# A two-layer hybrid diffusion backbone: the modulation products on the tensor engine's four column groups, the norm sums as matmuls, and a reordered start of each layer

## The chip, the core and the metric

One core of a Trainium2 chip runs the whole program. The metric is the device time of one execution in microseconds, as the median of several runs. The engines are called by the profile's names: PE (TensorE, with its weight loads as PEld), DVE (VectorE), ACT (ScalarE), POOL (GpSimd) and SP (SyncE, which only issues transfers).

## The reference, cut to what matters

There are two layers over 256 context tokens and 1024 latent tokens of width 1024. At the head of a layer each token is normalised and modulated by a vector that comes from a conditioning vector `c` (latent) or `c_ctx` (context). Three head groups then read the same projected input.

```python
for layer in range(DEPTH):                       # DEPTH = 2
    mod_x = jax.nn.silu(c) @ ada_w[layer] + ada_b[layer]        # 1024 -> 3072
    mod_c = jax.nn.silu(c_ctx) @ ada_w[layer] + ada_b[layer]
    sh_x, sc_x, gt_x = jnp.split(mod_x[:, None, :], 3, axis=-1)  # and the same of mod_c
    h_x = rmsnorm(x, norm_w[layer]) * (1.0 + sc_x) + sh_x
    h_c = rmsnorm(xc, norm_w[layer]) * (1.0 + sc_c) + sh_c
    y_x, y_c = hybrid_mixer(h_x, h_c, w_in[layer], ...)          # attention, GLA, HGRN2, out
    x = x + gt_x * y_x
    if layer < DEPTH - 1: xc = xc + gt_c * y_c
return rmsnorm(x, final_norm_w)
```

The modulation products are matrix-vector products: two vectors (`c` and `c_ctx`) times a 1024 x 3072 matrix for each layer, 12.6 MB of weights each.

## The kernel before, in words

Activations lie transposed: 8 tiles of 128 features (`KT`) by 1280 tokens (`NT`), the tokens in three chunks, A0 (256 context tokens), A1 and B (512 latent tokens each). `make_h` turns `x` into the modulated `h` as a pair, `hhi` rounded to the fast matmul format and `hlo` the remainder. A projection (`proj`) is three matmuls per feature tile (`hhi` by `whi`, `hlo` by `whi`, `hhi` by `wlo`), so 24 for a chunk and a block of 128 columns. The weights are split the same way by `split_w` on ACT and then DVE or POOL.

PE and SP run in the order in which the program is written. For DVE, ACT and POOL a scheduler sets the order at build time; each engine then runs its list in order. Most large tiles come from one pool of 34 slots ("big").

The start of layer 0: SP loads four rows of modulation weights (`ada_load`, 2.1 MB each, 512 columns), the first weights, and then `x`. `ada_row` multiplies a row on PE with `sil` (the two SiLU vectors, 2 columns) as the stationary operand into 2 partitions of `adps`, ACT copies it to `rows`, and `ada_cols` turns it into columns by matmuls with a 2 x 2 identity. The norm sums: ACT squares `x`, DVE and POOL add the squares into `acc` and `acc2` (`stats`), and `rstd` sums over partitions with one or two matmuls with a matrix of ones (`ssps`); `newton` refines the reciprocal root on ACT and DVE.

Then `gla` runs for the layer. Its small projection `gkp` and its blocks q, k, v and v2 are computed at once, chunk by chunk; after each chunk `run_side(SIDE)` takes three steps of `ada_side`, which computes the other modulation products: those of layer 1, needed only when layer 0 is done. Before the change these are 48 products of 128 x 1024 elements with a reduction, two thirds as one DVE instruction each (line 175), one third as a POOL product (line 171) and an ACT sum (line 172). `mids` is a list of steps that `gla` takes between its projections: in layer 0 the norm and `h` of chunk B and the two remaining rows of layer 0's modulation, in layer 1 the norm and `h` of chunk B (`mid_h`).

After q, k, v and v2 the scan of `gla` starts. From there on PE takes projections of later groups as fillers between the scan's steps; the first filler is the first PE work behind v2. The whole order of PE after that point is the same program before and after the change.

Of the kernel before, what the change touches and what calls it, by code (L numbers as in the profile page):

```python
# [65 lines left out]
def hybrid_kernel(ctx: ExitStack, tc: tile.TileContext, a: dict, out: bass.AP):  # L66
# [79 lines left out]
    sbc = [big(f"sbc{v}") for v in range(2)]  # L146
# [7 lines left out]
    def sbc_load():  # L154
        for v in range(2):
            cb, sv = big("cb")[:, 0:1024], sbc[v][:, 0:1024]
            nc.sync.dma_start(cb, a["cvec"][v].partition_broadcast(P))
# [4 lines left out]

    def ada_side():
        sbc_load()
        for i in range(8, 32):
# [833 lines left out]
    sil = const.tile([P, KT, 2], F32, name="sil")  # L999
    sigmul(sil, cvec)  # L1000
    xs = [big(f"x{k}") for k in range(KT)]
    adw = []
    def ada_load(i):
        w = []
        for j in range(4):
            w.append(big("adw0")[:, 0:1024].rearrange("p (k x) -> p k x", k=2))
            nc.sync.dma_start(w[j], a["ada_w"][i][:, 2 * j:2 * j + 2])
        return w

    for i in range(4):  # L1010
        adw.append(ada_load(i))
# [6 lines left out]
    rowt = big("rows")  # L1018
    rows = [rowt[0:2, 512 * (i % 2):512 * (i % 2) + 512] for i in range(6)]

    acc2 = big("acc2")

    def stats(c, xs=xs, acc=acc, acc2=acc2):
# [3 lines left out]
    def ada_cols(i):  # L1027
        pt = pst.tile([P, 512], F32, tag="t1", name="adtp")
        for j in range(4):
            nc.tensor.matmul(  # L1030
                pt[:, 2 * j:2 * j + 2], rows[i][:, j * P:(j + 1) * P], ident[0:2, 0:2], start=True, stop=True
            )
        if i < 4:
            m, b, d = m0, adab, (KT if i % 2 == 0 else 0) + 4 * (i // 2)
        else:
            m, b, d = m1, adab2, 4 * (i - 4)
        nc.vector.tensor_tensor(
            m[:, d:d + 4, :], pt[:, 0:8].rearrange("p (j v) -> p j v", v=2),
            b[:, d:d + 4].unsqueeze(2).to_broadcast([P, 4, 2]), op=ALU.add,
        )  # L1040

    def ada_row(i, w):
        ps = psp.tile([P, 512], F32, tag="pp", name="adps")
        for j in range(KT):
            nc.tensor.matmul(ps[0:2, :], sil[:, j, :], w[j // 2][:, j % 2, :], start=(j == 0), stop=(j == KT - 1))
        nc.scalar.copy(rows[i], ps[0:2, :])

    for i in range(4):
        ada_row(i, adw[i])
        if i > 0:  # L1050
            ada_cols(i - 1)
        if i in (1, 3):
            stats(CH_ALL[i // 2])
    rstd(r, acc, CH_ALL[0:1], acc2)
    ada_cols(3)
    hh = [big(f"hhi{k}", F32R) for k in range(KT)]
    hl = [big(f"hlo{k}", F32R) for k in range(KT)]
    As = [mod_gain(0, k, m0) for k in range(KT)]
    for k in range(KT):
# [4 lines left out]

    def starts(xs=xs, r=r, acc=acc, As=As, hh=hh, hl=hl):
        stats(CH_ALL[2])
        rstd(r, acc, CH_ALL[2:3], acc2)
        ada_row(4, ada_load(4))
        for k in range(KT):
# [310 lines left out]
```

## Time and profile before

| | us |
|---|---|
| median of 3 runs | 2010.65 |
| the runs | 2006.82, 2010.65, 2015.01 |
| span of the profiled execution, first to last instruction | 2006.4 |

The profile gives the span of one execution and not a time of its own beside it. It lies 0.4 us under the fastest run and 4.2 us under the median, so within the spread of the runs the span stands for the time. Over the span PE is busy 89%, DVE 68%, ACT 55% and POOL 27%. PE is the engine to watch: from about 200 us on it is busy nine tenths of the time or more in almost every slice, and the slices in which it is not lie at the start. The granted clock of PE has two levels, 2.4 and 1.2 GHz; a stretch with a share of 0.64 was at the lower level for most of its time. "Idle before" and a releaser in brackets say what an engine waited for.

### The profile page before, as it was taken

To read this page: it belongs to the slowest core of one execution; us is meant where nothing else is said; L and a number is where in the kernel's file an instruction comes from. 1 tells how busy PE (TensorE), PEld (TensorE's weight loads), DVE (VectorE), ACT (ScalarE), POOL (GpSimd) and SP (SyncE) were. 2 spreads that over 40 slices of the span, in tenths; PEclk is the share of its full clock that TensorE was granted. 3 is DMA by queue.
4 is the path that set the end of the run, shared out by engine and by line. 5 is a ranking of instruction groups with operands and counts; after the bars stand their busy time and mean duration, and the time that the engine had idled before them with its cause. 6 is when DMAs were issued, how large, how long until landed. Compare 5 with 4: busy or idle time off the path is not lost. (4 is left out here: it accounts for less than half of the span.)

```text
span 2006.4 us, 30011 instructions
## 1 busy us (share of the span) xinstructions
PE 1790.1 (89%) x10528; PEld 1408.4 (70%) x10528; DVE 1361.9 (68%) x2999; ACT 1105.6 (55%) x2891; POOL 543.3 (27%) x614
## 2 busy tenths in 40 slices
PE   7847898988989999997998988988898999999895
PEld 2436666766767788886887775666675777887775
DVE  2899847759475477678767666575838366677756
ACT  3634666457365367677634346545626355767633
POOL 1276223234243001111111333223434201111112
PEclk9878999989989999998999989999998999999997
DMA  9442112112114114416243011211211414246322
GB/s 337 151 149 100 38 48 95 48 46 85 63 42 119 48 61 115 143 64 196 96 150 129 26 40 45 84 49 48 98 66 50 114 51 119 79 123 198 102 94 84
DMA packets 81526, 190.28 MB, mean 95 GB/s; under 512 B 9408, under 2 KB 19904, under 8 KB 81376
## 3 DMA queue, kind: packets, MB, share of 16 engines
q1 hardware_dynamic: 44752, 101.72, 15.7%
q10 hardware_dynamic: 27936, 49.56, 6.8%
q0 software_dynamic: 8688, 37.10, 6.3%
q8 instruction: 83, 1.36, 0.3%
q14 instruction: 67, 0.55, 0.1%
HBM read 132.37 MB, written 45.48 MB: 89 GB/s over the span
## 5 line engine op out<-in xcount | busy, mean ns | idle before, releaser
L299 PE MATMUL pj<-hhi,whi 128*128 128x512 f32 (+1 forms) x1416 | 578.1, 408 | 8.5 <-ACT sg L317 5.7
L301 PE MATMUL pj<-hhi,wlo 128*128 128x512 f32 (+1 forms) x1416 | 536.5, 379 | 13.9 <-DVE wlo L276 11.4
L300 PE MATMUL pj<-hlo,whi 128*128 128x512 f32 (+1 forms) x1416 | 536.8, 379 | 0.0
L299 PEld LDWEIGHTS pj<-hhi,whi 128*128 128x128 f32 x1416 | 275.6, 195 | 73.9 <-issue 25.0
L301 PEld LDWEIGHTS pj<-hhi,wlo 128*128 128x128 f32 x1416 | 276.3, 195 | 70.4 <-DVE wlo L276 12.0
L300 PEld LDWEIGHTS pj<-hlo,whi 128*128 128x128 f32 x1416 | 276.5, 195 | 36.8 <-issue 2.7
L276 POOL TENSOR_TENSOR wlo<-wst,whi 128x512 fp32r<-128x512 f32 x80 | 112.9, 1412 | 494.7 <-ACT whi L275 456.1
L275 ACT CAST whi<-wst 128x512 fp32r<-128x512 f32 x144 | 84.4, 618 | 139.6 <-PE pj L300 99.6
L960 DVE TENSOR_TENSOR PT<-ptp,PT 128x384 fp32r<-128x384 f32 (+2 forms) x272 | 119.4, 466 | 34.9 <-ACT PT L959 32.8
L943 DVE CUSTOM_DVE_ANT_0 sp<-sps,tab 128x640 f32<-128x640 f32 (+2 forms) x144 | 107.4, 746 | 44.5 <-PE sps L937 41.7
L959 ACT CAST PT<-ptp 128x384 fp32r<-128x384 f32 (+2 forms) x272 | 101.6, 409 | 61.9 <-PE ptp L957 58.9
L944 ACT ACTIVATE sp<-sp,mn 128x640 f32<-128x640 f32 (+2 forms) x144 | 111.5, 774 | 41.1 <-DVE mn L943 39.5
L957 PE MATMUL ptp<-cst,sp 128*128 128x128 f32 x640 | 101.1, 282 | 19.8 <-DVE PT L960 8.1
L957 PEld LDWEIGHTS ptp<-cst,sp 128*128 128x128 f32 x640 | 78.1, 144 | 40.7 <-DVE PT L960 9.7
L970 PE MATMUL pv<-PT,nv 128*128 128x256 f32 x640 | 105.2, 293 | 0.0
L936 PE MATMUL sps<-k,q 128*128 128x256 f32 (+1 forms) x272 | 86.5, 323 | 11.9 <-DVE mn L943 11.3
L276 DVE TENSOR_TENSOR wlo<-wst,whi 128x512 fp32r<-128x512 f32 x64 | 53.5, 836 | 63.2 <-ACT whi L275 62.7
L970 PEld LDWEIGHTS pv<-PT,nv 128*128 128x128 f32 x640 | 91.0, 192 | 6.4
L317 ACT ACTIVATE sg<-pj 128x512 f32<-128x512 f32 (+1 forms) x90 | 47.9, 533 | 83.0 <-PE pj L301 82.6
L1146 DVE SCALAR_TENSOR_TENSOR xn<-py,m,xn 128x512 f32<-128x512 f32 (+1 forms) x88 | 56.9, 650 | 39.9 <-PE py L1141 38.3
L937 PE MATMUL sps<-k,q 128*128 128x256 f32 (+1 forms) x272 | 78.9, 309 | 0.0
L574 ACT COPY zg<-swg 32x64 f32<-32x64 f32 x216 | 52.0, 241 | 32.4 <-PE lv L589 24.0
(303 smaller groups left out, 3893.0 us busy)
## 6 DMA issues: line engine op xcount, KB each, us to landing
wst<-in_w_in SPq DMA_DIRECT2D x128, 256.0 KB, 3.1
pre<-sg ACTq DMA_DIRECT2D x80, 256.0 KB, 2.0
adw<-in_ada_w SPq DMA_DIRECT2D x24, 512.0 KB, 9.9
adw<-in_ada_wt SPq DMA_DIRECT2D x24, 512.0 KB, 3.5
k<-k POOLq DMA_DIRECT2D x32, 320.0 KB, 4.4
tab<-in_rpbt SPq DMA_DIRECT2D x16, 640.0 KB, 6.0
wst<-in_w_out SPq DMA_DIRECT2D x32, 256.0 KB, 3.5
oscr<-sg ACTq DMA_DIRECT2D x24, 256.0 KB, 2.0
```

The costliest lines, as they stand in the source:

```text
L275: nc.scalar.copy(hi, st)
L276: (nc.vector, nc.gpsimd)[WPOOL[h]].tensor_tensor(lo, st, fence(hi), op=ALU.subtract)
L299: nc.tensor.matmul(ps[:, :n], hi[:, k, :], mv(hh[k]), start=(k == 0), stop=False)
L300: nc.tensor.matmul(ps[:, :n], hi[:, k, :], mv(hl[k]), start=False, stop=False)
L301: nc.tensor.matmul(ps[:, :n], lo[:, k, :], mv(hh[k]), start=False, stop=(k == KT - 1))
L936: nc.tensor.matmul(sps[:, pc:pc + w], Q1[h][:, qc:qc + P], K1[h][:, kc:kc + w], start=True, stop=False)
L943: nc.vector.tensor_tensor_reduce(sp, sps[:, c0:c0 + n], tab[:, tb:tb + n], -1.0, 3.0e38, ALU.add, ALU.min, mn)
L944: nc.scalar.activation(sp, sp, AF.Exp, bias=mn, scale=-1.0, accum_out=sm)
L957: nc.tensor.transpose(pt[:, j * P:(j + 1) * P], sp[:, (b0 + j) * P:(b0 + j + 1) * P], ident)
L959: nc.scalar.copy(PT[:, b0:b0 + bn, 0, :], p3)
L960: nc.vector.tensor_tensor(PT[:, b0:b0 + bn, 1, :], p3, fence(PT[:, b0:b0 + bn, 0, :]), op=ALU.subtract)
L970: nc.tensor.matmul(pv[:, i % 2], V[h][:, c, :], st[i]["PT"][:, j], start=(j == 0), stop=(j == len(chs) - 1))
```

## The change

It does five things.

1. `ada_side` multiplies on PE. A step loads a chunk of 256 columns (`ada_w2`, two transfers of 0.5 MB), and `ada_mm` does 8 matmuls with 32 stationary columns each (2 of the vectors, 30 zeros), feature tile j into the column group 32 * (j % 4) of `adps`, so that four groups hold four partial sums. ACT copies 128 x 256 to `rows`, and `ada_fold` sums the groups and turns the row into columns with 2 matmuls against `sel`. There are 16 chunks: layer 1's modulation and the last third of layer 0's, which had been rows 4 and 5 of `mids`. The DVE, POOL and ACT products are gone.
2. Layer 0's first four rows use `ada_mm` and `ada_fold` with 512 columns.
3. `stats` sums the squares on PE: 8 matmuls with the matrix of ones per chunk in place of additions on DVE and POOL.
4. ACT's queue issues the loads of chunks A0 and A1 of `x`, A0 ahead of the first modulation row, A1 behind it; chunk B stays on SP behind the weights. Two of the eight feature tiles of `h` in layer 0 (`HPOOL0`) take a product and a subtraction on POOL.
5. `gla` projects chunk A0 of q and k before `gkp` of chunk A1, takes the second step of `mids` only after q of chunk A1, and has k's weights loaded ahead of time. This holds for layer 1 too.

```diff
-    sbc = [big(f"sbc{v}") for v in range(2)]
+    rowt = big("rows")
+    sil = rowt[:, 1024:1280].rearrange("p (k x) -> p k x", x=32)
+    nc.gpsimd.memset(sil, 0.0)
...
+    def ada_mm(ps, ws, n):
+        for j in range(KT):
+            g = 32 * (j % 4)
+            nc.tensor.matmul(
+                ps[g:g + 32, :n], sil[:, j, :], ws[j], start=(j < 4), stop=(j >= 4), skip_group_check=True
+            )
+
+    def ada_fold(row, n, m, b, d):
+        pt = pst.tile([P, 512], F32, tag="t1", name="adtp")
+        w = n // P
+        for j in range(w):
+            nc.tensor.matmul(pt[:, 2 * j:2 * j + 2], row[:, j * P:(j + 1) * P], sel, start=True, stop=True)
...
     def ada_side():
-        sbc_load()
-        for i in range(8, 32):
-            w = big("adw")[:, 0:1024]
-            nc.sync.dma_start(w, a["ada_wt"][i - 8])
-            for v in range(2):
-                if (2 * i + v) % ADAM < ADAP:
-                    t = big("adt")[:, 0:1024]
-                    nc.gpsimd.tensor_tensor(t, w, sbc[v][:, 0:1024], op=ALU.mult)
-                    nc.scalar.activation(t, t, AF.Copy, accum_out=m1[:, i, v:v + 1])
-                else:
-                    t = sgt().bitcast(BF16)
-                    nc.vector.scalar_tensor_tensor(
-                        t, w, 1.0, sbc[v][:, 0:1024], op0=ALU.mult, op1=ALU.mult, accum_out=m1[:, i, v:v + 1]
-                    )
...
+        ws = load(0)
+        for c in range(16):
+            nxt = load(c + 1) if c < 15 else None
+            ps = psp.tile([P, 512], F32, tag="pp", name="adps")
+            ada_mm(ps, ws, 256)
+            row = rowt[:, 256 * (c % 4):256 * (c % 4) + 256]
+            nc.scalar.copy(row, ps[:, 0:256])
             yield
+            ada_fold(row, 256, m1, adab2, 2 * c)
+            ws = nxt
+            yield
...
         gkp(CH_A[0:1])
         next(mids)
+        if CH_A[0] in chunks:
+            run(wq, CH_A[0:1], q, sq)
+        run(wk, CH_A[0:1], k)
         gkp(CH_A[1:2])
+        run(wq, CH_A[1:2], q, sq)
         next(mids)
-        wk = load_split(a["w_in"][l, GLK])
-        run(wq, [c for c in chunks if c in CH_A], q, sq)
-        next(mids, None)
-        run(wk, CH_A, k)
+        run(wk, CH_A[1:2], k)
         gkp(CH_B)
...
+    x_load(nc.scalar, 0)
+    adw = [ada_load(0)]
+    x_load(nc.scalar, 1)
+    adw += [ada_load(i) for i in (1, 2, 3)]
     pw = gla_weights(0)
-    for s, n in CH_ALL:
-        for k in range(KT):
-            nc.sync.dma_start(xs[k][:, s:s + n], a["xin"][:, k, s:s + n])
+    x_load(nc.sync, 2)
...
+    def stats(c, acc=acc, r=r, xs=xs):
+        s, n = CH_ALL[c]
+        ps = pst.tile([P, 512], F32, tag="t1", name="ssps")
         for k in range(KT):
-            stat((acc, acc2)[k % 2], xs[k], k // 2, *c, eng=(nc.vector, nc.gpsimd)[k % 2])
+            sq = sgt()[:, :n]
+            nc.scalar.activation(sq, xs[k][:, s:s + n], AF.Square)
+            nc.tensor.matmul(ps[:, :n], ones, sq, start=(k == 0), stop=(k == KT - 1))
...
+    stats(0)
+    row = ada_row(0)
+    stats(1)
+    for i in range(4):
+        nrow = ada_row(i + 1) if i < 3 else None
+        ada_fold(row, 512, m0, adab, (KT if i % 2 == 0 else 0) + 4 * (i // 2))
+        row = nrow
+        if i % 2 == 1:
+            ks = range(2 * (i - 1), 2 * (i - 1) + 4)
+            for k in ks:
+                As[k] = mod_gain(0, k, m0)
+            h_part(0, ks)
+    h_part(1, range(KT))
```

The order of ACT at the very start, before:

```order
L1366 UNCONDITIONAL_BRANCH
L231 ACT_TABLE_LOAD
L149 ACTIVATE sil<-smalls 128x16
L134 ACTIVATE lbe<-lbe 128x8
L1046 COPY rows<-adps 2x512 x2
L708 CAST wg<-gkst 128x8x32
L275 CAST whi<-wst 128x512
```

and with the change (rows 9 to 21 of its list; the first loads of chunk A0 stand ahead of them):

```order
L1019 DMA x_125<-in_xin 128x256
L1019 DMA x_126<-in_xin 128x256
L1019 DMA x_127<-in_xin 128x256
L1019 DMA x_120<-in_xin 128x512
L1019 DMA x_121<-in_xin 128x512
L1019 DMA x_122<-in_xin 128x512
L1019 DMA x_123<-in_xin 128x512
L1019 DMA x_124<-in_xin 128x512
L1019 DMA x_125<-in_xin 128x512
L1019 DMA x_126<-in_xin 128x512
L1019 DMA x_127<-in_xin 128x512
L1042 ACTIVATE sg<-x_120 128x256
```

All sixteen loads of chunks A0 and A1 now stand ahead of ACT's first square (line 1042), and PE's first matmul needs that square.

On PE behind the first projection of q (chunk A0) in layer 0, with the change; `adps` is a chunk's product, `adtp` its fold:

```order
L314 MATMUL pj<-hhi_219,wlo 128x256
L159 MATMUL adps<-adw,rows 32x256 x8
L167 MATMUL adtp<-smalls,rows 128x2 x2
L159 MATMUL adps<-adw,rows 32x256 x8
L312 MATMUL pj<-hhi_212,whi 128x256
```

where DVE, in the same stretch of the program before the change, had the products (line 175) between the work of `gla` itself (`glf` and `glk` are its decay and its key):

```order
L276 TENSOR_TENSOR wlo<-wst,whi 128x512
L744 TENSOR_TENSOR glf_957<-glf_957,glu 128x256
L175 SCALAR_TENSOR_TENSOR sg,m_111<-adw,sbc_113 128x1024
L175 SCALAR_TENSOR_TENSOR sg,m_111<-adw,sbc_114 128x1024
L743 TENSOR_SCALAR glf_957<-zps,smalls 128x512
L765 TENSOR_TENSOR glk_413<-glk_413,rsh 128x1024
```

The products have left DVE's list, and PE's has a product and a fold directly behind one another, with ACT's copy of the product between them.

On PE in layer 1, around the norm sum of chunk B (`ssps`), before:

```order
L720 MATMUL pj<-hhi_10160,wg 128x512
L721 MATMUL pj<-hlo_10168,wg 128x512
L202 MATMUL ssps<-acc,cst 128x512
L299 MATMUL pj<-hhi_10153,whi 128x512
L300 MATMUL pj<-hlo_10161,whi 128x512
```

and with the change:

```order
L313 MATMUL pj<-hlo_10244,whi 128x512
L314 MATMUL pj<-hhi_10236,wlo 128x512
L215 MATMUL ssps<-acc,cst 128x512
L312 MATMUL pj<-hhi_10229,whi 128x512
L313 MATMUL pj<-hlo_10237,whi 128x512
```

The sum stood behind `gkp` of chunk A1 (wg), ahead of q's A1 and both of k's chunks; it now stands behind q's A1, with k's A1 alone between it and `gkp` of chunk B.

## Rows read from the trace of the kernel before

**Rows 1.** Busy time by stretch: us; PE, PEld, DVE, ACT, POOL busy (instructions); clock, DMA, GB/s

```profile
20.00:40.00 20.00, 20.00 (x59) 5.28 (x58) 6.07 (x13) 7.99 (x19) 5.00 (x5) 1.00 0.97 343
...
100.00:125.00 25.00, 19.78 (x76) 15.76 (x75) 24.15 (x17) 8.73 (x16) 23.43 (x8) 0.86 0.39 125
125.00:150.00 25.00, 5.03 (x15) 2.84 (x14) 25.00 (x26) 7.04 (x14) 14.89 (x6) 0.64 0.51 177
...
175.00:200.00 25.00, 19.00 (x89) 16.90 (x89) 25.00 (x35) 9.47 (x23) 18.59 (x13) 0.84 0.26 84
```

**Rows 2.** Groups by line and shape, 0 to 215 us: count, busy us, mean ns, idle before

```profile
L175 DVE SCALAR_TENSOR_TENSOR sg<-adw,sbc 128x1024 bf16<-128x1024 f32 x32 | 64.5, 2062 | 2.3 <-POOL sbc L161 2.3
L171 POOL TENSOR_TENSOR adt<-adw,sbc 128x1024 f32<-128x1024 f32 x16 | 49.7, 3122 | 13.3 <-DMA adw<-in_ada_wt 11.9 <-ACT adt L172 1.3
...
L225 DVE SCALAR_TENSOR_TENSOR x<-x,modA,rstd 128x512 f32<-128x512 f32 x16 | 11.8, 807 | 0.0
L227 DVE SCALAR_TENSOR_TENSOR hlo<-x,m,hhi 128x512 fp32r<-128x512 f32 x16 | 10.8, 740 | 0.0
...
L227 DVE SCALAR_TENSOR_TENSOR hlo<-x,m,hhi 128x256 fp32r<-128x256 f32 x8 | 5.5, 725 | 0.0
...
L225 DVE SCALAR_TENSOR_TENSOR x<-x,modA,rstd 128x256 f32<-128x256 f32 x8 | 4.3, 607 | 0.0
```

**Rows 3.** What PE waited for between 100 and 205 us: us, times, longest

```profile
PE zps L737 <- DVE glf L743: 20.0, 1, 20.0
PE pj L301 <- DVE wlo L276: 11.2, 2, 6.0
```

**Rows 4.** Timeline of the start: start, us, engine, line, operation

```profile
7.64 16.43 PE L1045 MATMUL adps<-adw,sil 128*2 128x512 f32 x32 [7.64 <-DMA adw<-in_ada_w]
...
24.98 7.03 PE L1045 MATMUL adps<-adw,sil 128*2 128x512 f32 x16
...
31.94 1.05 PE L1030 MATMUL adtp<-cst,rows 2*128 2x2 f32 x8
...
33.11 0.72 ACT L192 ACTIVATE acc<-x 128x256 f32<-128x256 f32 x2
```

**Rows 5.** Timeline: ACT's copy of `gkp` A0, then a 256-column projection on PE

```profile
62.94 0.37 ACT L722 COPY gk<-pj 128x256 f32<-128x256 f32 x1 [2.57 <-PE pj L721]
...
86.25 0.28 PE L299 MATMUL pj<-hhi,whi 128*128 128x256 f32 x1
86.36 0.28 PE L300 MATMUL pj<-hlo,whi 128*128 128x256 f32 x1
```

**Rows 6.** End of `gla`'s projections in layer 0: ACT's copies of v, the first filler

```profile
L751 ACT ACTIVATE vT<-pj x6: 384/580/597, 154.2 to 188.5; 128x512 f32<-128x512 f32 x4, 128x256 f32<-128x256 f32 x2
...
194.44 0.58 PE L301 MATMUL pj<-hhi,wlo 128*128 128x256 f32 x1 [6.00 <-DVE wlo L276]
```

**Rows 7.** Timeline, PE: the scan's matmuls into 32-column groups, layer 0

```profile
213.06 0.45 PE L589 MATMUL lv<-zg,zkg 128*32 128x64 f32 x16
...
215.42 0.43 PE L589 MATMUL lv<-zg,swg 128*32 128x128 f32 x8
```

**Rows 8.** Timeline of layer 1's start, PE, DVE, POOL and ACT

```profile
1110.84 0.39 PE L720 MATMUL pj<-hhi,wg 128*128 128x512 f32 x1
1111.07 0.39 PE L721 MATMUL pj<-hlo,wg 128*128 128x512 f32 x1
1111.55 1.12 PE L202 MATMUL ssps<-acc,cst 128*128 128x512 f32 x2
...
1117.34 5.85 DVE L225 SCALAR_TENSOR_TENSOR xn<-xn,modA,rstd 128x512 f32<-128x512 f32 x7
...
1124.24 4.06 DVE L227 SCALAR_TENSOR_TENSOR hlo<-xn,m,hhi 128x512 fp32r<-128x512 f32 x6
...
1124.40 5.01 POOL L223 TENSOR_TENSOR hlo<-xn,hhi 128x512 fp32r<-128x512 f32 x1 [5.73 <-DVE xn L222]
...
1131.84 0.59 ACT L722 COPY gk<-pj 128x512 f32<-128x512 f32 x1 [4.71 <-PE pj L721]
```

More of the change, by code (lines that the diff above doesn't have):

```diff
@@ L114, in hybrid_kernel @@
     cvec = take(KT, 2)
+    sel = take(2)
     adab = take(16)
@@ new lines, in ada_fold, with load @@
+    def ada_fold(row, n, m, b, d):
[3 more added lines that the diff above has]
+            nc.tensor.matmul(pt[:, 2 * j:2 * j + 2], row[:, j * P:(j + 1) * P], sel, start=True, stop=True)
+        nc.vector.tensor_tensor(
+            m[:, d:d + w, :], pt[:, 0:2 * w].rearrange("p (j v) -> p j v", v=2),
+            b[:, d:d + w].unsqueeze(2).to_broadcast([P, w, 2]), op=ALU.add,
+        )
+    def ada_side():
+        def load(c):
+            ws = []
+            for j in range(2):
+                t = big("adw")[:, 0:1024].rearrange("p (k x) -> p k x", k=4)
+                nc.sync.dma_start(t, a["ada_w2"][c][:, 4 * j:4 * j + 4])
+                ws += [t[:, k] for k in range(4)]
+            return ws
+        ws = load(0)
[5 more added lines that the diff above has]
+            nc.scalar.copy(row, ps[:, 0:256])
@@ L997, in na_run, with x_load @@
         return oT
-    sil = const.tile([P, KT, 2], F32, name="sil")
-    sigmul(sil, cvec)
+    sigmul(sil[:, :, 0:2], cvec)
     xs = [big(f"x{k}") for k in range(KT)]
-    adw = []
+    def x_load(eng, c):
+        s, n = CH_ALL[c]
+        for k in range(KT):
+            eng.dma_start(xs[k][:, s:s + n], a["xin"][:, k, s:s + n])
     def ada_load(i):
@@ L1005, in ada_load @@
         for j in range(4):
-            w.append(big("adw0")[:, 0:1024].rearrange("p (k x) -> p k x", k=2))
-            nc.sync.dma_start(w[j], a["ada_w"][i][:, 2 * j:2 * j + 2])
-        return w
-    for i in range(4):
-        adw.append(ada_load(i))
+            t = big("adw0")[:, 0:1024].rearrange("p (k x) -> p k x", k=2)
+            nc.sync.dma_start(t, a["ada_w"][i][:, 2 * j:2 * j + 2])
+            w += [t[:, 0], t[:, 1]]
+        return w
+    x_load(nc.scalar, 0)
+    adw = [ada_load(0)]
@@ L1012, in hybrid_kernel @@
+    x_load(nc.scalar, 1)
+    adw += [ada_load(i) for i in (1, 2, 3)]
     pw = gla_weights(0)
-    for s, n in CH_ALL:
-        for k in range(KT):
-            nc.sync.dma_start(xs[k][:, s:s + n], a["xin"][:, k, s:s + n])
+    x_load(nc.sync, 2)
     acc = big("acc")
     r = big("rstd")
[L1018 to L1023, printed above, removed]
+    def stats(c, acc=acc, r=r, xs=xs):
+        s, n = CH_ALL[c]
+        ps = pst.tile([P, 512], F32, tag="t1", name="ssps")
@@ L1024, in stats @@
         for k in range(KT):
-            stat((acc, acc2)[k % 2], xs[k], k // 2, *c, eng=(nc.vector, nc.gpsimd)[k % 2])
[L1027 to L1055, printed above, removed]
+            sq = sgt()[:, :n]
@@ L1061, in hybrid_kernel, with h_part @@
-    rstd(r, acc, CH_ALL[1:2], acc2)
-    for k in range(KT):
-        make_h(xs[k], r, As[k], m0, k, hh[k], hl[k], CH_ALL[1:2])
-    def starts(xs=xs, r=r, acc=acc, As=As, hh=hh, hl=hl):
[L1066 to L1069, printed above, removed]
-            make_h(xs[k], r, As[k], m0, k, hh[k], hl[k], CH_ALL[2:3])
+    As = [None] * KT
+    def h_part(c, ks, xs=xs, r=r, As=As, hh=hh, hl=hl):
+        for k in ks:
+            make_h(xs[k], r, As[k], m0, k, hh[k], hl[k], CH_ALL[c:c + 1], HPOOL0)
@@ new lines, in ada_row @@
+    def ada_row(i):
+        row = rowt[:, 512 * (i % 2):512 * (i % 2) + 512]
+        ps = psp.tile([P, 512], F32, tag="pp", name="adps")
+        ada_mm(ps, adw[i], 512)
+        nc.scalar.copy(row, ps)
+        return row
+    stats(0)
[7 more added lines that the diff above has]
+            ks = range(2 * (i - 1), 2 * (i - 1) + 4)
+            for k in ks:
+                As[k] = mod_gain(0, k, m0)
+            h_part(0, ks)
```

36 lines of the change are left out of this document (12 added, 24 removed).

## The prediction

> **What bounds the kernel now.** I read four views in this order. First the busy time by stretch [rows 1]: between 100 and 200 us PE is busy 19.8, 5.0 and 19.0 us in 25, at shares of the clock of 0.86, 0.64 and 0.84, while DVE is full (24.2 to 25.0 of 25). So ahead of 200 us the kernel waits for DVE, and behind it for PE. Second the groups by line [rows 2]: what fills DVE there are the 32 products of line 175, 64.5 us, and on POOL the 16 of line 171, 49.7 us. Third what PE waited for [rows 3]: one wait of 20.0 us for `glf`, which stands in DVE's list behind such products, and 11.2 us in two waits for `wlo`. Fourth the timeline of the start [rows 4]: PE works on modulation rows from 7.6 to 32.0 us, folds until 33, and only then does ACT square `x`, which came last on the queue. Then `gkp` of A0 is copied at 62.9 [rows 5], the last block of v leaves PE at about 188, and the first filler starts at 194.4 after a wait of 6.0 for `wlo` [rows 6]. The order of PE's work from that filler to layer 1 is the same in both kernels, and PE is nearly full there, so what is won at the filler is taken as won at the end, and what layer 1's start loses is lost. The span, 2006.4 us, is within the spread of the runs; I apply the difference to the median, 2010.65.
>
> **Prices.** Matmuls of 512 columns in the fast format follow one another every .23 us (1110.84 and 1111.07 [rows 8]), those of 256 every .11 to .12 [rows 5]. A 512-column matmul in full fp32 is two records of .44 each (16 records in 7.03 us [rows 4]). For four column groups the nearest row is the scan's: 16 records of 64 columns into 32-column groups in .45 us, 8 records of 128 in .43 [rows 7]. Sixteen records of 64 columns one after the other would at the speed of rows 4 be .88; so about half of it or more overlaps. I take full overlap of four: a row of 512 columns then is 4 x .44 = 1.8 us instead of 7.0, a chunk of 256 columns .9. A change from the fast format to fp32 costs .25 (.48 instead of .23 ahead of `ssps` [rows 8]). A fold of two matmuls is .5, half of the 1.05 for four [rows 4].
>
> A rule of the Trainium skill speaks against this part: "TensorEngine Tiling (Array Packing)", Key Properties, says that changing the tiling mode drains TensorE. The scan of this kernel does change modes, and rows 7 show groups only inside such stretches, so the trace does not give the drain apart. "TensorE: Matmul & The Clock Gate", Part 3, has three column tiles measured at 2.38 times one, from which I estimate 3.2 times for four: a chunk would be 1.1 us and the sum some 4 us later.
>
> **Layer 0, the start.** ACT's list now has all 16 loads of A0 and A1 ahead of its first square. Bounds for that square: when A0's 1 MB is there (at 343 GB/s [rows 1] 3 us plus a start of 1.5, so 5 us), or when all of A0, row 0 and A1 has landed (5.2 MB, 17 us). I take 17, since the issues stand ahead of it. On SP the loads of A0 and A1 fall away, rows 1 to 3 move up, and B stays behind the first weights; B's sums come 80 us later, so that order costs nothing. The chain is then: sums of A0 until 23 (8 fp32 matmuls of 256 columns, 3.5 us, twice that at half clock, behind the squares), row 0 until 25, sums of A1 until 33 (8 x .88 = 7.0), row 1, a fold, row 2 and a fold until 39. The data of row 3 (11.5 MB in all) are there at about 35, not later. Then DVE: its list mixes A0 and A1, six tiles each, two being on POOL: 6 x (.607 + .725) + 6 x (.807 + .740) = 17.3 [rows 2], less 1.8 begun earlier, plus 6 for the gains, `wg` and one or two `wlo`: 21.5. POOL's two tiles, with 5.0 for a subtraction [rows 8] and about half of 3.1 for a product [rows 2], need at most 2 x 6.6 for A1 and half of it for A0, 20, and lie beside that. So `gkp` of A0 is done at about 60 instead of 62.9, but now with A1's `h` done as well, and gkp, q and k run on without the old gaps.
>
> **Layer 0, from there to the first filler.** PE's own work: 224 matmuls of 512 columns (24 for each of four blocks and two chunks, 32 for `gkp`) x .23 = 51.5; 96 of 256 x .118 = 11.3; five `zps` of .86 (two records of .43) 4.3; the 8 for the sums of B, 7.0; together 74.1. Added: 16 chunks x (.88 + .5) = 22.1 and 11 calls of `run_side` with two changes of format each, 22 x .25 = 5.5: 27.6. The two old rows 4 and 5 (2 x 7.0) and the 20.0 and 6.0 us of waiting are gone with DVE's 64.5.
>
> A new wait comes with the change: in each of the 11 calls a fold stands directly behind its product, with ACT's copy between (.37 [rows 5] and a start, .6), and PE's queue behind the fold waits too: 6.6; where ACT is in a copy of v (.38 to .60 [rows 6]) more, 3. Together 9.6; bounds 0, if ACT's copy were hidden, and 20, if each stood behind two such copies. The loads of the chunks (1 MB each some 10 us, 100 GB/s) lie beside this; the queue has carried 343 [rows 1].
>
> A second new wait: `gkp` of B needs B's `h`. In layer 1 the last `hlo` ends on POOL 16.7 us after `ssps` (1112.67 to 1129.41) and `gkp`'s copy begins 2.4 later: 19.1 [rows 8]. The same chain in layer 0 has as cover k's A1 (5.5), a side call (2.5) and `gkp` itself (3.7): 7.4 us are left, and with the clock, which was at .64 in the stretch with the 20 us wait [rows 1], I take 8; bounds 0, if DVE, free now, does the chain in 12, and 12.
>
> Sum: 60 + 74.1 + 27.6 + 9.6 + 8 = 179.3; the filler starts at about 180 instead of 194.4: **a gain of about 14.5**.
>
> **Layer 1.** There is no modulation here, only the new order. `ssps` of chunk B stood ahead of q's A1 and of k's A0 and A1; now q's A1 (24 x .23 = 5.5) and k's A0 (24 x .118 = 2.8) come ahead of it. `gkp` of B is already bound by `h` in the trace of before (19.1 behind `ssps`, a wait ahead of the copy of 4.71 on ACT's side [rows 8]), so it moves by the whole 8.3; nothing else fills PE. A wait of that length lowers the clock for what follows; between 0 and 3.7 (`gkp` of B at half clock), I take 1.2. **Loss about 9.5**, bounds 5 (if free POOL and DVE shorten the chain) and 12.
>
> Net: 14.5 - 9.5 = 5 to 6 us, so **about 2005**.
>
> **The rivals.**
> 1. Both new waits hide: the copy and `h` of B cost half in layer 0, 9 us less, and the row of 60 stands. Then 2005 - 9 = 1996; with both gone 1987.5. For it: DVE, which was full between 100 and 200 us [rows 1], loses 64.5 us of work, so its chain may run faster than in layer 1. Against: in layer 1 DVE has no products either, and the 16.7 are measured there.
> 2. Slower: the groups do not overlap in fp32, since the two records of one matmul follow each other and the next group's must keep its turn. It decides from the point where a chunk takes more than about 1.7 us. By strict order with one neighbour overlapping, a chunk is 9 x .22 = 2.0 instead of .9, for 16 chunks 17 us, and a row 4.0 instead of 1.8, 9 us in four, of which perhaps half is on the path: 2005 + 17 + 4 = 2026. Against it: rows 7, where 16 records take .45 us. For it: those records are of 64 columns, and no row has groups at 256 or 512. The Trainium skill ("TensorE: Matmul & The Clock Gate", Part 3, The mechanism) has matmuls strictly in order in start and end, which would give this; rows 7 as they stand do not look like it.
> 3. Slower at the start: row 0 and the sums of A1 shift because ACT's first square comes at 22 to 26 us (the loads of A1 share the transfers with rows 1 to 3). All of the start then moves by 5 to 9 us and nothing takes it up: 2010 to 2014.
> 4. The change does not do what it says: the chunks' loads come late and PE waits for them, as it did at the start [rows 4]; 16 x 1 us, 2021. Little speaks for it.
>
> **How the numbers follow.** My forecast (net gain 0 to 10) has .45, rival 1 .33, rival 2 .10, rival 3 .09, rival 4 .03. The time is that of the forecast, 2005. The range goes from 1990 (nearly all of both waits hidden, or a shorter loss in layer 1) to 2021; below lie some .08, above some .11. A difference under .5%, 10 us, is about what measuring can't tell from none: faster means under 2000.6, slower over 2020.7. Rival 1 gives .33 of faster and the forecast's edge a little, .34; slower is rival 2, with parts of 3 and 4 and of sums that go wrong together, .17; the rest, .49, the same.
>
> **What would show it.** In the profile after: a row `adps` of 512 columns near 1.8 us and a chunk near .9 to 1.1 (rival 2: 2.0); the first square near 17 us (rival 3: 22 or more); ACT's copy of `gkp` A0 near 60; no product on DVE; PE's waits in layer 0 for ACT's `rows` copy, some 10 us in 11 to 16 places, and at `gkp` of B for `hlo`, 5 to 8; the first filler near 180; in layer 1 the stretch from the end of `ssps` to the copy of `gkp` B still near 19 us, with a wait of PE of 7 to 10 in it that before was 1 or 2. I am wrong if the filler starts before 172 or after 188, if layer 1's start loses under 5, or if PE's work behind the filler takes another time in the new kernel.

## The result, and the profile after

The changed kernel takes 2026.24 us (median of 4 runs, 2024.11 to 2029.73), beside 2009.91 for the kernel before in the same comparison: a ratio of 1.0085, 95% interval 1.0069 to 1.0102. It is slower by 16 us, where 5 to 6 us faster was forecast, and lies above the range of 1990 to 2021. The profiled execution has a span of 2023.3 us, against 2006.4, so the two traces differ by 16.9 us.

The busy time by stretch of the kernel after answers to [rows 1]; the columns are the same:

```profile
20.00:40.00 20.00, 18.44 (x76) 9.72 (x80) 2.46 (x7) 11.69 (x24) 1.42 (x2) 1.00 0.87 341
40.00:60.00 20.00, 9.29 (x65) 5.65 (x57) 20.00 (x37) 12.09 (x23) 9.21 (x6) 0.67 0.46 155
60.00:80.00 20.00, 15.52 (x117) 12.85 (x118) 4.83 (x12) 4.28 (x10) 3.19 (x2) 0.73 0.50 176
80.00:100.00 20.00, 17.55 (x86) 10.88 (x85) 0.16 (x1) 4.24 (x8) 0.00 (x0) 0.91 0.44 151
100.00:125.00 25.00, 21.14 (x83) 14.05 (x82) 15.68 (x20) 9.36 (x16) 6.91 (x4) 0.80 0.58 199
125.00:150.00 25.00, 20.18 (x145) 13.87 (x143) 12.36 (x15) 10.54 (x23) 8.13 (x4) 1.00 0.34 115
```

The bound has moved as the change's parts suggest. DVE, full from 100 to 200 us before, works 12 to 16 us in each 25 between 100 and 150 us and 0.16 us between 80 and 100, and PE is busy in these stretches. PE is the engine that the others wait for, but at a clock of 0.67 to 0.91 between 40 and 125 us.

What PE waited for between 66 and 192 us (us, times, longest) answers to [rows 3]:

```profile
PE adtp L167 <- ACT rows L188: 6.0, 9, 1.5
PE adtp L167 <- DVE m L168: 2.4, 1, 2.4
PE pj L734 <- DVE hlo L240: 2.3, 2, 1.9
PE adtp L167 <- ACT whi L288: 2.0, 1, 2.0
PE adps L159 <- DMA adw<-in_ada_w: 2.0, 1, 2.0
...
```

The waits of 20.0 us for `glf` and 11.2 us for `wlo` are gone. The folds (`adtp`) wait 6.0 + 2.4 + 2.0 = 10.4 us instead, nearly the 9.6 forecast.

The timeline of the start, which answers to [rows 4, 5]: start, us, engine, line, operation:

```profile
5.06 15.46 ACTq L1019 DMA_DIRECT2D x<-in_xin  x11
...
20.57 1.03 ACT L1042 ACTIVATE sg<-x 128x256 f32<-128x256 f32 x3 [15.31 <-DMA x<-in_xin]
...
21.04 6.34 PE L1043 MATMUL ssps<-sg,cst 128*128 128x256 f32 x16 [21.04 <-ACT sg L1042]
...
36.82 1.92 PE L159 MATMUL adps<-adw,rows 128*32 128x512 f32 x16
...
44.35 1.95 PE L167 MATMUL adtp<-smalls,rows 128*128 128x2 f32 x16
...
66.02 0.37 ACT L735 COPY gk<-pj 128x256 f32<-128x256 f32 x1 [4.00 <-PE pj L734]
```

ACT issues the last eleven loads of `x` from 5.06 to 20.5 us and can do nothing else in that time; its first square comes at 20.57, and PE's first matmul at 21.04 (7.64 before). A row of 512 columns takes 1.92 us on four column groups. The last fold of the four rows ends at 46.3 and `gkp` of A0 is copied at 66.02, 3.1 us later than before.

The first filler starts at 191.18, with no wait ahead of it:

```profile
190.95 0.39 PE L314 MATMUL pj<-hhi,wlo 128*128 128x512 f32 x1
191.18 0.28 PE L312 MATMUL pj<-hhi,whi 128*128 128x256 f32 x1
...
191.41 0.28 PE L314 MATMUL pj<-hhi,wlo 128*128 128x256 f32 x1
```

The row of 194.44 in [rows 6] is not the filler's first matmul but its third, the one that needs `wlo`; the first had started at 188.05 before. Like for like, the third now stands at 191.41, so PE is 3.0 us ahead there.

Layer 1's start answers to [rows 8]: first what PE waited for (1103 to 1155 us), then rows of PE, ACT's copies and the clock (the last column but two of the stretch):

```profile
PE pj L733 <- DVE wg L722: 6.3, 1, 6.3
PE pj L734 <- DVE hlo L240: 3.4, 1, 3.4
PE pj L734 <- POOL hlo L236: 2.4, 1, 2.4
PE pj L733 <- ACT hhi L239: 1.9, 1, 1.9
```

```profile
1123.13 1.02 PE L215 MATMUL ssps<-acc,cst 128*128 128x512 f32 x2
1131.50 0.49 PE L733 MATMUL pj<-hhi,wg 128*128 128x512 f32 x1 [1.87 <-ACT hhi L239]
1135.38 0.80 PE L734 MATMUL pj<-hlo,wg 128*128 128x512 f32 x1 [3.39 <-DVE hlo L240]
...
1142.38 0.63 PE L733 MATMUL pj<-hhi,wg 128*128 128x512 f32 x1
1142.81 0.63 PE L734 MATMUL pj<-hlo,wg 128*128 128x512 f32 x1
...
1145.18 0.59 ACT L735 COPY gk<-pj 128x512 f32<-128x512 f32 x1 [9.36 <-PE pj L734]
```

```profile
1135.00:1145.00 10.00, 7.26 (x16) 4.82 (x17) 4.76 (x8) 0.82 (x2) 5.02 (x1) 0.50 0.00 0
```

The wait of 6.3 us for `wg` was there before, too. In `gkp` of chunk B PE waits 1.9 + 3.4 + 2.4 = 7.7 us, where it waited 1.4 before, and its matmuls follow each other every .43 us (1142.38, 1142.81) instead of .23, at a clock of 0.50, the lower level.

Where the 16.9 us lie follows from the same PE instruction in both traces (time after minus time before, each from its span's start, at the given time of before; PE's order is the same from the first filler on but for layer 1's start):

| at (us) | 205 | 222 | 270 | 440 | 470 | 600 | 790 | 1080 | 1140 | 1300 | 1340 | 1980 |
|---|---|---|---|---|---|---|---|---|---|---|---|---|
| after - before | -5.0 | -1.2 | 0.0 | 0.0 | +4.0 | +0.7 | +3.8 | +3.8 | +13.8 | +13.1 | +15.7 | +16.9 |

So layer 0's start and the first part of its scan end even, the rest of layer 0 adds 3.8, the start of layer 1 adds 10.0 and what follows 3.1.

### The profile page after: what moved, and what is told of

Same layout as the page of the kernel before. It is cut to its first block, busy times and chain, and to the rows that moved or that the text cites. A ratio compares the mean times of both kernels' runs of the same rounds, so it can differ in the third digit from the quotient of the medians.

```text
span 2023.3 us, 30512 instructions
## 1 busy us (share of the span) xinstructions
PE 1798.0 (89%) x10836; PEld 1427.0 (71%) x10836; DVE 1281.2 (63%) x2933; ACT 1088.8 (54%) x2867; POOL 492.3 (24%) x600
## 5 line engine op out<-in xcount | busy, mean ns | idle before, releaser
L950 PE MATMUL sps<-k,q 128*128 128x256 f32 (+1 forms) x272 | 86.9, 324 | 11.7 <-DVE mn L957 11.2
```

Of the source, the lines that this page charges most:

```text
L950: nc.tensor.matmul(sps[:, pc:pc + w], Q1[h][:, qc:qc + P], K1[h][:, kc:kc + w], start=True, stop=False)
```

## The experiments

All ratios are to the kernel before, with a 95% interval; the change itself is 1.0085.

**e1: layer 1 with the old place of the norm.** The condition on the layer stands around three lines of `gla`:

```diff
-        run(wk, CH_A[0:1], k)
+        if l == 0:
+            run(wk, CH_A[0:1], k)
         gkp(CH_A[1:2])
+        if l == 1:
+            next(mids)
         run(wq, CH_A[1:2], q, sq)
-        next(mids)
-        run(wk, CH_A[1:2], k)
+        if l == 0:
+            next(mids)
+        run(wk, CH_A[1:2] if l == 0 else CH_A, k)
```

> The changed kernel, but in layer 1 alone the norm of chunk B is taken right behind gkp of A1 again, with q's A1 and k's A0 and A1 behind it; layer 0 is as changed. My theory: the new order costs layer 1's start 10 us by itself (the gkp of chunk B waits 7.6 us instead of 1.4 for h, and then runs at the lower clock), so the time falls from 2026 to about 2016, with the wait ahead of gkp B in layer 1 back to 1 to 2 us. Rival: the 10 us come from something that the change left in layer 1 besides the order (ACT's or POOL's lists); then the time stays within 3 us of 2026.

2012.04 us, 1.0010 (0.9995 to 1.0026): 14 us back. The waits of PE at layer 1's start are those of before:

```profile
PE pj L733 <- DVE wg L722: 6.3, 1, 6.3
PE pj L734 <- POOL hlo L236: 1.4, 1, 1.4
...
```

Between 1080 and 1140 us this trace neither loses nor gains against before (0.0), where the changed kernel loses 10.0. The other 4 us are partly the spread of the runs and partly small shifts in layer 0's later scans and at 1340 us, which differ from build to build. The rival falls.

**e2: folds one product later.**

```diff
-            ada_fold(row, 256, m1, adab2, 2 * c)
+            if c > 0:
+                ada_fold(prow, 256, m1, adab2, 2 * c - 2)
+            prow = row
...
+        ada_fold(prow, 256, m1, adab2, 30)
+        yield
```

> The changed kernel, but each fold of a 256-column chunk is put behind the product of the next chunk, so that it no longer stands right behind its own product and ACT's copy. Theory: the waits of PE for the copy (10.4 us between 66 and 192 us, up to 2.4 each) go, and with them the stretches at the lower clock that follow the longer ones; the last block of v ends 10 to 14 us earlier, and the time is 2014 to 2018. Rival A: the copies only wait elsewhere (ACT is late anyway and PE waits at the next step), then under 4 us. Rival B: the scan's first steps hang on DVE and ACT and not on PE's arrival, so that PE's gain ahead of the scan is given back in it; then the last v is early but the time stays near 2022 to 2026.

2024.89 us, 1.0080 (1.0053 to 1.0107): 1.4 us, no difference. The waits of the folds for ACT's copy are gone, but `gkp` of B, with its waits for `h`, now takes 11.9 us against 10.6 (it starts 3.3 us earlier and ends 1.9 earlier), and 2.7 us of waiting stand elsewhere; the first filler is 1.4 us earlier, and that is lost in the scan. In this execution q of A0 starts 2.1 us later than in the changed kernel (67.90 against 65.78), so from there to the filler 3.5 us are won. Rivals A and B each hold in part: other waits take the place of a good half of the folds', and the rest isn't seen at the end.

**e3: the loads of `x` by SP.**

```diff
-    x_load(nc.scalar, 0)
+    x_load(nc.sync, 0)
...
-    x_load(nc.scalar, 1)
+    x_load(nc.sync, 1)
```

> The changed kernel, but the loads of chunks A0 and A1 of x are issued by SP in the same order among the modulation rows, not by ACT. Theory: ACT's first square waited until 20.6 us only because ACT was held while it issued loads (5.1 to 20.5 us); now it begins at 5 to 8 us, the sums of A0 are done by 15, the sums of A1 by 25, the last fold of the four rows at 37 to 39 instead of 46.3, and gkp of A0 is copied at about 59 instead of 66.0; the time falls by 5 to 7 us to about 2020. Rival: the transfers themselves set the start (the last row's data land at 42 us in any order), then the last fold moves by under 2 us and the time stays within 2 us of 2026.

2018.52 us, 1.0045 (1.0030 to 1.0061): 8 us back. The timeline of this kernel, first ACT's first square and PE's sums, then the copy of `gkp` A0:

```profile
4.82 0.42 ACT L1042 ACTIVATE sg<-x 128x256 f32<-128x256 f32 x1 [0.60 <-DMA x<-in_xin]
...
5.29 5.77 PE L1043 MATMUL ssps<-sg,cst 128*128 128x256 f32 x16 [5.29 <-ACT sg L1042]
...
19.00 8.83 PE L1043 MATMUL ssps<-sg,cst 128*128 128x512 f32 x16 [2.42 <-ACT sg L1042]
...
56.98 0.37 ACT L735 COPY gk<-pj 128x256 f32<-128x256 f32 x1 [4.00 <-PE pj L734]
```

The square starts 15.8 us earlier and `gkp` of A0 is copied 9.0 earlier: the loads on ACT's queue had set the start, and with the same bytes on SP's it comes earlier. Of the 9 us only 3 are left at the first filler, since in this build ACT's list has another order: ACT stands 10 us before `e16g`, which needs DVE's scan of the decay, with the copy of a product behind it, and the fold waits 7.3 for that copy (2.4 in the changed kernel):

```profile
132.36 1.14 ACT L288 CAST whi<-wst 128x512 fp32r<-128x512 f32 x2
143.63 0.34 ACT L480 ACTIVATE e16g<-glf 128x80 f32<-128x80 f32 x1 [10.13 <-DVE glf L476]
...
145.42 0.35 ACT L188 COPY rows<-adps 128x256 f32<-128x256 f32 x1
```

The traces then stay 3.2 us apart up to 1340 us; the other 3.7 us by which this execution ends earlier arise behind that point, where the edit changes nothing, and aren't explained.

**e4: one column group.** All eight matmuls of a product go to the first group, and copy and fold take 32 partitions.

```diff
-            g = 32 * (j % 4)
             nc.tensor.matmul(
-                ps[g:g + 32, :n], sil[:, j, :], ws[j], start=(j < 4), stop=(j >= 4), skip_group_check=True
+                ps[0:32, :n], sil[:, j, :], ws[j], start=(j == 0), stop=(j == KT - 1)
             )
...
```

> The changed kernel, but the eight matmuls of a modulation product go into one column group, one behind the other; copy and fold take 32 partitions. Theory: the four groups do run side by side, so without them a row of 512 columns takes 7.0 us instead of 1.92 and a chunk of 256 columns 3.5 instead of 1.07; 16 chunks are 39 us more and four rows up to 20 us more, of which the loads hide a part; the time is about 2070 to 2085. Rival: the groups save little, because the records' lengths are modelled and PE is held elsewhere; then under 2040.

2066.87 us, 1.0285 (1.0263 to 1.0307). A row and a chunk of this kernel on PE, then a chunk of the changed one with its fold:

```profile
28.89 7.05 PE L158 MATMUL adps<-adw,rows 128*32 128x512 f32 x16
...
79.55 3.64 PE L158 MATMUL adps<-adw,rows 128*32 128x256 f32 x16
```

```profile
70.93 1.07 PE L159 MATMUL adps<-adw,rows 128*32 128x256 f32 x16
72.55 0.61 PE L167 MATMUL adtp<-smalls,rows 128*128 128x2 f32 x4 [0.55 <-ACT rows L188]
```

7.05 against 1.92 and 3.64 against 1.07: four groups run 3.7 and 3.4 times as fast as one. The 16 chunks take 16 x 2.57 = 41 us more, and the four rows bring q of A0 9.6 us later (75.33 against 65.78); some 6 us of waits and of lower clock go in return, and the profiled execution is 45 us longer than that of the change (41 by the medians). The prediction's second rival falls. Nor does the drain at a change of tiling mode show that the prediction held possible: the product at 70.93 starts .24 us behind the last matmul ahead of it (70.69), and those before follow one another every .21 to .22.

**e5: e1's and e3's edits together.**

> The changed kernel with both earlier edits: the loads of x by SP, and in layer 1 the norm of chunk B ahead of q's A1. Theory: the two losses lie at different places and add up; the edits took 14 and 8 us alone, so 22 together, 2004. Rival: what the start wins is given back in the scan of layer 0, as it partly was (9 us at gkp A0, 3 at the end of v in the trace of the run with SP's loads), and the sum is under 16 us, over 2010.

2003.82 us, 0.9976 (0.9963 to 0.9989). The two add up, and the kernel is faster than before by 0.2%, with an interval that leaves out 1 by 0.1%. The fold's wait of 7.3 us for ACT's copy is here as in e3.

**e6: the old order in both layers.** `gkp` A1 and the norm of B stand directly behind `gkp` A0 again, then q and k.

```diff
-        if CH_A[0] in chunks:
-            run(wq, CH_A[0:1], q, sq)
-        run(wk, CH_A[0:1], k)
         gkp(CH_A[1:2])
-        run(wq, CH_A[1:2], q, sq)
         next(mids)
-        run(wk, CH_A[1:2], k)
+        run(wq, [c for c in chunks if c in CH_A], q, sq)
+        run(wk, CH_A, k)
```

> The changed kernel with the order of gla's projections of before in both layers (gkp A0, gkp A1, norm of chunk B, q's A0 and A1, k's A0 and A1, gkp B); loads, products, folds and sums stay as changed. Against the run that took the order back in layer 1 alone (2012): if the new order helps layer 0, as it should where A1's h is late, this is 3 to 6 us slower, 2015 to 2018. If it costs there too, because the norm of chunk B starts later and its h holds gkp B, it is 2 to 5 us faster, 2007 to 2010. Between 2010 and 2014 the order does not matter in layer 0.

2015.76 us, 1.0028 (1.0016 to 1.0041), 3.7 us over e1, with intervals that overlap. The number is the forecast's, the way to it isn't: with the old order `gkp` of B takes 3.9 us without a wait (10.3 in e1), and at the first block of v PE is 2.1 us ahead of e1 (143.44 against 145.53). It falls back at the fold behind that block, which waits 5.5 us (2.4 in e1) since ACT's list has the copy behind `e16g` again; at the second block PE is 3.9 us behind (157.82 against 153.95). Whether the new order helps layer 0 isn't shown.

**e7: PE kept busy.** 15 matmuls in full fp32, whose results nobody reads, in the waits of `gkp` of A0 and B.

```diff
+        def warm(dp, w):
+            for _ in range(w):
+                nc.tensor.matmul(dp, ones, cst[:, 0:4, :], start=True, stop=True)
...
+                w = {0: {0: 3, 8: 4, 9: 4, 13: 2}, 768: {1: 2}}.get(s, {}) if l == 0 else {}
...
```

> The changed kernel with 15 matmuls of 512 columns in full fp32 added in layer 0, whose results nobody reads: 13 in gkp of A0 at the four places where PE waited for h (2.8, 4.0, 4.3 and 2.3 us) and 2 in gkp of B. They are short enough to end within the waits at the higher clock. Theory: the clock fell because PE waited at these places; kept busy, it runs q's A0 in 2.8 us instead of 5.2 and gkp B in 4 to 6 us plus its wait instead of 10.5, and PE's work up to the end of v is 3 to 7 us shorter; the time falls by 2 to 6 us. Rival: the clock does not follow these waits, or the chain of h sets the pace there anyway; then q's A0 stays at 5 us and the time at 2026 or a little above.

2023.99 us, 1.0075 (1.0054 to 1.0096), 2 us less than the change, within the spread. The first matmuls of q's A0 in the changed kernel, then in this one:

```profile
65.78 0.41 PE L312 MATMUL pj<-hhi,whi 128*128 128x256 f32 x1
66.00 0.41 PE L313 MATMUL pj<-hlo,whi 128*128 128x256 f32 x1
```

```profile
68.14 0.28 PE L312 MATMUL pj<-hhi,whi 128*128 128x256 f32 x1
68.26 0.28 PE L313 MATMUL pj<-hlo,whi 128*128 128x256 f32 x1
```

```profile
60.00:80.00 20.00, 18.15 (x132) 12.23 (x131) 7.45 (x17) 6.98 (x15) 3.21 (x2) 1.00 0.64 226
```

They follow every .12 us instead of .22; the block takes 3.0 us instead of 5.2, and the clock between 60 and 80 us is 1.00 instead of 0.73. So the lower clock in that block does come from PE's waits before it. In `gkp` of B two such matmuls were too few (9.8 us against 10.6). From q of A0, which starts 2.4 us later in this execution, to the first block of v 3.3 us are won; but ACT's list has the copy behind `e16g` here too, the fold waits 7.3 us, and at the second block of v PE is 5.3 us behind the changed kernel. The time therefore doesn't tell what the saved 3 us are worth.

**e8: q and k of A0 inside `gkp` A0's waits,** on top of e5: three accumulators, filled tile by tile (`pg`, `pq`, `pk`), with two calls of `run_side` behind them.

```diff
+            for j in range(KT):
+                fi, la = j == 0, j == KT - 1
+                nc.tensor.matmul(pg[:, :n0], wg[:, j, :], th, start=fi, stop=False)
+                nc.tensor.matmul(pq[:, :n0], wq[0][:, j, :], th, start=fi, stop=False)
+                nc.tensor.matmul(pk[:, :n0], wk[0][:, j, :], th, start=fi, stop=False)
...
```

> As the run with both edits (SP's loads, layer 1's old place of the norm), and in layer 0 gkp, q and k of chunk A0 are computed tile by tile together, into three accumulators, so that the 6 us of q and k fall into the waits of gkp A0 for h. Theory: gkp A0 took 16.9 us in every run because it is paced by DVE's h, and PE had room for q and k in it; PE reaches gkp A1 5 to 7 us earlier, and the time is 3 to 6 us under that run, about 1999. Rival: A1's h or the later chain through DVE's decay and ACT sets the end of v, and nothing is left of it: within 2 us.

2005.46 us, 0.9981 (0.9967 to 0.9995): no difference to e5, though for another reason than the rival's. The joint block itself waits 7.3 us for `wlo`, and `gkp` of A1 starts 3.0 us later than in e5 (72.75 against 69.79). At 205 us PE is 5.8 us ahead of e5, but what brings it there is the fold behind the first block of v: it waits 0.8 us here and 7.3 in e5. At 1980 us 1.4 us are left, in an execution that was the fastest of the ten (1999.6).

**e9: the sums of B on DVE and POOL,** on top of e5.

```diff
+    acc2 = big("acc2")
+    for k in range(KT):
+        stat((acc, acc2)[k % 2], xs[k], k // 2, *CH_ALL[2], eng=(nc.vector, nc.gpsimd)[k % 2])
...
-        stats(2)
+        rstd(r, acc, CH_ALL[2:3], acc2)
```

> As the run with both edits (SP's loads, layer 1's old place of the norm; 2004), but the squares of chunk B in layer 0 are added on DVE and POOL again, as before the change, with two matmuls of sums left on PE instead of 16 records. Theory: PE's 8.8 us for these sums (at 84 to 93 us in that run) lay in the middle of a stretch in which PE was the engine that all waited for and DVE had under 1 us of work in 20, so moving them to PE cost what they take: here the sums take 1 to 2 us, the end of v comes 6 to 7 us earlier, and the time is 1996 to 1999. Rival: the norm's own chain sets gkp B, and with an earlier sum PE only waits longer there for h: under 2 us.

1998.63 us, 0.9952 (0.9934 to 0.9970), 5 us under e5. PE's sums of B in the changed kernel, then here:

```profile
94.14 8.83 PE L1043 MATMUL ssps<-sg,cst 128*128 128x512 f32 x16
```

```profile
91.53 2.08 PE L215 MATMUL ssps<-acc,cst 128*128 128x512 f32 x2
93.40 1.91 PE L217 MATMUL ssps<-acc,cst 128*128 128x512 f32 x2
```

The sums take 2.8 us up to the next block instead of 8.3. But PE comes to them 7.5 us later than in e5 (91.53 against 84.05; the loads of the chunks alone make it wait 4.9 us instead of 1.7), and at the first block of v it is still 1.9 us behind (135.43 against 133.58). What puts it ahead is the fold behind that block, in e5 and then here:

```profile
PE adtp L167 <- ACT rows L188: 7.3, 1, 7.3
```

```profile
PE adtp L167 <- ACT glu L755: 0.8, 1, 0.8
```

So the end of v comes 6.4 us earlier, as forecast, but by luck, since ACT's list has the copy ahead of `e16g` in this build. What the sums cost on PE is not shown.

**e10: as e9, and the norm of B taken ahead of `gkp` A1 in layer 0.**

```diff
         if l == 0:
             run(wk, CH_A[0:1], k)
+            next(mids)
         gkp(CH_A[1:2])
...
-        if l == 0:
-            next(mids)
```

> As e9, and layer 0 takes the norm of chunk B between k's A0 and gkp of A1, not behind q's A1. Theory: h of chunk B is then ready when gkp of B begins; the waits there (about 4 us) and the stretch at the lower clock behind them (gkp B took 10.1 us, 3.9 at the higher clock) go, 4 to 6 us less than e9. Rival: DVE, ACT and POOL, which now do this chain at the same time as the end of A1's h, come too late for gkp A1, which then waits as long: within 2 us of e9.

1997.31 us, 0.9944 (0.9921 to 0.9967), 1.3 us under e9: within the spread, as the rival has it, but not for its reason. `gkp` A1 doesn't wait, and `gkp` of B takes 3.9 us instead of 8.9, at the full clock:

```profile
100.86 0.40 PE L733 MATMUL pj<-hhi,wg 128*128 128x512 f32 x1
101.09 0.40 PE L734 MATMUL pj<-hlo,wg 128*128 128x512 f32 x1
```

```profile
100.00:125.00 25.00, 21.99 (x130) 15.48 (x130) 5.71 (x13) 9.03 (x19) 3.04 (x2) 1.00 0.43 161
```

At the first block of v PE is 9.4 us ahead of e9, at the second 3.6: most of what was won went into the folds' waits for ACT's copy, 11.8 us here and 6.9 in e9, the longest of them (4.4) again for the copy behind `e16g`, and into the lower clock behind it.

**e11: as e10, with e2's edit.**

> As e10, with each fold put behind the next chunk's product. In the changed kernel this alone took 1 us of some 8 us of waits that it removed, since PE then waited at gkp B. Theory: where gkp B no longer waits, the removed waits (6 to 9 us) become time, 3 to 6 us less than e10. Rival: as before, other waits take their place: within 2 us.

1992.58 us, 0.9916 (0.9892 to 0.9940), 4.7 us under e10. By the medians the edit is worth 1.4 us on the changed kernel (e2) and 4.7 here, but each is a median of four runs that lie 7 to 10 us apart; between q of A0 and the filler the traces give 3.5 and 4.6 us. This version is faster than both kernels: by 0.8% than the one before, by 1.7% than the changed one.

**One place in ACT's list.** The list of ACT is ordered anew in every build. In e3, e5, e6, e7 and e10 it has the copy of one product behind `e16g`, and the fold waits 4.4 to 7.3 us for it; in the change, e1, e8 and e9 that fold waits 0.8 to 2.4. The place lies between the first block of v (chunk A0) and the second (A1). PE's start there, less that of the run compared with (us), tells what an edit wins ahead of it from what the list adds:

| | first block of v | second block of v | third matmul of the filler |
|---|---|---|---|
| e3 less the change | -9.9 | -3.6 | -3.2 |
| e5 less e1 | -12.0 | -5.7 | -5.4 |
| e6 less e1 | -2.1 | +3.9 | +4.1 |
| e7 less the change | -0.9 | +5.3 | +4.2 |
| e8 less e5 | +2.4 | -3.8 | -5.8 |
| e9 less e5 | +1.9 | -4.4 | -6.4 |
| e10 less e9 | -9.4 | -3.6 | -2.9 |
| e11 less e10 | -3.0 | -5.6 | -5.6 |

A shift of about 6 us there is as large as most of the differences under test. No run holds ACT's order fixed, so it stays open what e3 to e10 would give without it.

## Why the prediction was wrong

**What held.** The price of the column groups (1.92 us for a row, forecast near 1.8; 1.07 for a chunk, forecast .9 to 1.1), and with it the verdict on rival 2: the scan's rows of 64 and 128 columns [rows 7] carry over to 256 and 512. The Trainium skill ("TensorE: Matmul & The Clock Gate", Part 3, Measured speedup vs the span model) gives 2.38 for three groups, from which I had estimated 3.2 for four; 7.05 over 1.92 is 3.7. The side work is also right in sum: from q of A0 to the first filler the products with the waits behind them took 29.3 us and the folds 7.8, together 37.1, where 27.6 + 9.6 = 37.2 was forecast. That it is so close is luck: the waits are 12.4 us (10.4 of the folds, 2.0 for a load) instead of 9.6, and the work is 24.7 instead of 27.6. The loss in layer 1 is right in size, place and cause: 9.5 forecast, 10.0 measured, the stretch from the end of `ssps` to the copy being 21.0 us (1124.15 to 1145.18) where 19 was forecast; the lower clock, set down with 1.2, took some 3.6 of it (half of the 7.26 us of busy time between 1135 and 1145; an estimate). e1 shows it by taking it away.

**The step that failed is layer 0's sum:** "the filler starts at about 180", a gain of 14.5. It started at 191.2, a gain of 3.2 by the row that the prediction took, and by 270 us that was gone. Two terms were mis-sized by 6 us each. Of the 21.9 us between the forecast's net gain of 5.0 and the loss of 16.9, 11.3 lie ahead of the filler, 3.2 between there and 270 us, 0.5 in layer 1's start and 3.8 + 3.1 in the later shifts of the table, whose cause is open.

*The start,* 60 for `gkp` of A0; it was 66.0. The bounds for ACT's first square were 5 and 17 us, and I took 17 "since the issues stand ahead". It came at 20.6, above the upper bound, since ACT was held until its last load was issued (20.5). An issue itself takes .33 to 1.26 us; ahead of those at 9.59, 13.05, 19.21 and 20.19 ACT stands still, 9.7 us in all, and in the trace each of the four starts .02 to .03 us behind the landing of an earlier load of `x`, while SP's rows land in between. So the third rival's mechanism (5 to 9 us, with .09) is there: A1's loads share the transfers with the rows, and ACT has to wait them out. In the five other builds that load so (e1, e2, e4, e6, e7) PE's first matmul comes later still, at 23.1 to 24.1 us instead of 21.0. e3 shows what it is worth: 9 us at `gkp` A0, 3 at the filler, and 8 of the whole by the medians. The lower bound, 5 us, is what SP's queue gives (4.82), though for the first of A0's eight tiles alone; the start of 1.5 us in it is in no row.

*PE's own work from there to the filler,* 74.1 us plus 8 of waiting for `h` of B; it was 86.0 plus 2.3. The wait was priced too high and the work too low. The counts were right, the speed wasn't: about 10 of the 11.9 us are matmuls at the lower clock. q of A0 took 5.2 us instead of 2.8, `gkp` of B 8.2 without its waits instead of 3.7, the sums of B 8.3 instead of 7.0, and the first latent chunk of v that follows the fold wait of 2.4 us 7.35 instead of 5.6. Two matmuls of `gkp` of B, .43 us apart instead of .23:

```profile
118.35 0.63 PE L734 MATMUL pj<-hlo,wg 128*128 128x512 f32 x1
118.78 0.63 PE L733 MATMUL pj<-hhi,wg 128*128 128x512 f32 x1
```

I had priced the clock with .6 us in layer 0, taken from a single wait of 20 us [rows 1], while the change puts many waits of 1.5 to 4 us into PE's list. e7 shows for q's A0, and e10 for `gkp` of B, that the clock is up when PE has no long wait ahead.

**"What is won at the filler is taken as won at the end"** holds only in part. All builds that I compared so lose 3 to 5 us against before between 205 and 222 us, where the scan's first steps go from DVE to PE to ACT and back and PE's earlier arrival, as I read it, doesn't help (`l` waits for DVE's `zg` and for ACT, 6.9 us in all after 190 us). e2 and e8 gave back what they had won; e9 and e11 kept most of theirs (15.0 and 22.9 us at 205, 9.5 and 16.2 at 1980). The remaining shifts, +3.8 in the later scans of layer 0 and +3.1 in layer 1's, appear in some builds and not in others (at 1080 us less at 270 us: +3.8 in the change, +0.4 in e1, +2.5 in e9, +0.5 in e7), while PE's order there is the same; which of the rearranged instructions on ACT, DVE or POOL makes them was not tried and stays open.

**Part by part,** then: the new order costs layer 1 ten us (e1); what it does to layer 0 is not shown, since ACT's list changed with it (e6). The loads on ACT's queue cost 9 to 12 us up to v, of which that same list took 6 back, and 8 of the whole by the medians (e3, e5). What the sums of B cost on PE is not shown (e9). The products on four groups run at the price forecast (e4). With the first two costs taken out the kernel is 0.2% faster than the one before (e5), and the best version 0.8% (e11).

## What to carry to other kernels

Before a difference is put down to an edit, compare the two traces at several instructions that both have: here ACT's list, ordered anew by the scheduler, moved PE by 6 us behind the place of the edit, and once that was the whole gain. Before work is moved to the engine that will be the bound, ask which engine has the time: the products left a full DVE, while the sums of B went to PE where DVE had 0.16 us of work in 20; whether moving them back pays is not shown. Price a moved projection at the clock which the waits ahead of it leave, not at the clock of the dense stretch. And a single wait that is removed shows little while another stands behind it (e10: 9.4 us at the first block of v, 2.9 at the filler); take them out together before deciding.

## What the runs showed of the hardware

The queue of an engine that also computes is no free place for loads: eleven issues of 128 or 256 KB held ACT for 15.5 us (5.06 to 20.5), 9.7 of them standing still until an earlier load had landed, while issued by SP the same loads let ACT square at 4.8 us. Waits of 2 to 4 us, several close together, were enough for the lower level of PE's clock (0.50 over 1135 to 1145 us, 0.73 over 60 to 80), and a few matmuls without use in them kept it at 1.00 over 60 to 80. A wait of 2.4 us (at 148 to 151) was followed by the lower level as well (0.50 over 152.7 to 156). Eight fp32 matmuls of 512 columns over four column groups took 1.92 us and in one group 7.05.
